# Moving an S5 parameter chain to GpSimd, its output factors to VectorE, and six weight splits into quarters, in a two-layer decoder trunk

## The chip, the cores and the metric

The kernel runs on one core of a Trainium2 chip. The metric is the device time of one launch in microseconds (us), as the median of several runs. The engines of the core are named as in the profile: PE (TensorE, matrix products), PEld (its weight loads), DVE (VectorE), ACT (ScalarE), POOL (GpSimd) and SP (SyncE, which issues the DMAs here). Each engine works through its own queue strictly in order; semaphores hold an instruction until what it reads is there.

## The reference, cut to what matters

The trunk has two residual layers over 1024 positions of width 1024. Layer 0 runs sliding-window attention and an S5 state-space mixer side by side off one input projection; layer 1 is an indexed sparse attention. The change touches the S5 mixer of layer 0 and the preparation of weights.

```python
def s5_mixer(u, log_dt, a_re, a_im, b_re, b_im, c_re, c_im, d_skip, glu_w, glu_b):
    ug = u.reshape(bsz, L, G, W // G)
    dt = jnp.exp(log_dt)[:, None]
    mag = jnp.exp(a_re * dt)
    ang = a_im * dt
    ab_re = mag * jnp.cos(ang)
    ab_im = mag * jnp.sin(ang)
    den = a_re * a_re + a_im * a_im
    n_re = ab_re - 1.0
    n_im = ab_im
    f_re = (n_re * a_re + n_im * a_im) / den
    f_im = (n_im * a_re - n_re * a_im) / den
    bb_re = f_re[..., None] * b_re - f_im[..., None] * b_im
    ...
    bu_re = jnp.einsum('blgh,gph->blgp', ug, bb_re)
    ...
    _, _, x_re, x_im = lax.associative_scan(ssm_combine, (at_re, at_im, bu_re, bu_im), axis=1)
    y = (jnp.einsum('blgp,ghp->blgh', x_re, c_re) - jnp.einsum('blgp,ghp->blgh', x_im, c_im) + d_skip * ug)
    y = jax.nn.gelu(y.reshape(bsz, L, W))
    h = y @ glu_w + glu_b
    return h[..., :W] * jax.nn.sigmoid(h[..., W:])
```

All products with weights are in float32 accuracy: the kernel splits each weight and each activation into a rounded part (hi) and a remainder (lo) and sums three products.

## The kernel before, in words

**Order of the work.** The program is written in one order, and a planner places each engine's instructions by priority (earlier in the program is higher) and by its own estimate of when each is ready; what it fixes is the order in each engine's queue. So an instruction written later can stand earlier in a queue where the planner expects a gap.

**Layer 0, start.** The input comes in eight pieces of 128 rows. For each, ACT rounds it (L336), DVE takes the remainder (L337), ACT squares it (L341), and a running sum of squares is kept (L343, on POOL for pieces 1 and 2, else on DVE). PE meanwhile forms the first chunk of the projection (L357 to L359). Then `mean_square` (L203 to L211) sums over partitions on PE (L208), and takes 1 / rms as a power of -0.5 on POOL (L211); DVE spreads it over a diagonal `dg` (L365), PE multiplies that with ones (L368) and ACT copies the product to `rb` (L369).

**S5's parameters** (L435 to L539) are tiles of 128x16 numbers, all on DVE except the two sines on ACT (L454, L457): `exp_of` (L240 to L253) is an exponential as a polynomial; it gives dt and mag. Angle, its reduction to one turn and the sine and cosine follow, then the input factors `Bb` (L459 to L473, L534 to L539), the powers `pw` of the step (L490 to L500), the table `ue` of powers of the unit rotation, each made by `square` (L493) and straightened by `unit` (L505), and the first 16 steps `T16` of the rotation (L517 to L528).

**Quarters of S5.** `s5_quarter` (L589 to L710) runs four times. Each builds on DVE the input weights `Q` (L613 to L618) and a rotation table `Tb` of 128 steps (L634 to L639), and on POOL the output factors `W` (L620 to L627) by `cmul` (L598 to L610), which four DMAs bring into `Wp` (L632). PE transposes `Q` (L646), multiplies it with the input (L674), DVE rotates the result, runs the scans (L687) and writes the states `X` (L678 to L698). PE then forms the output from `M` and U (L705) and from `Wp` and `X` (L707). `Q`, `W`, `Wp`, `Tb` and `X` have one buffer each. Between and beside the quarters the planner places the other projections of layer 0: keys and values (`proj_rows`, L218 to L220, and `norm_heads`, L383 to L394, whose 1 / rms is on POOL, L199 and L200), the second S5 input chunk, the queries (`q_chunk`, L396) and the gates (`gate_chunk`, L411, `proj_cols`, L232 to L234).

**Weights.** `load_w` (L135) brings each of 39 weight pieces of 128x2048 in; ACT rounds it (L153) and DVE or POOL subtracts (L154). The list `LO_ON_V` says which pieces DVE takes. Pieces of DVE, and of POOL those numbered 21, 31 and 32, are done in steps of 2 of 8 rows (128x512), the others whole (128x2048) where they are flushed at once; from piece 21 on a projection paces the steps itself.

Of the kernel before, what the change touches and what calls it, by code (L numbers as in the profile page):

```python
# [8 lines left out]
F32 = mybir.dt.float32  # L9
# [59 lines left out]
def tile_hybrid_swa_s5_dsa(  # L69
# [56 lines left out]
    LO_ON_V = (0, 1, 2) + tuple(range(13, 21)) + (29, 30) + tuple(range(33, 39))  # L126
# [8 lines left out]
    def load_w(src):  # L135
# [19 lines left out]
        return (hi, lo), [piece, WSTEP if i in LO_ON_V or i in (21, 31, 32) else 8, 0]  # L155
# [39 lines left out]
    last_rstd = [None]  # L195
# [7 lines left out]
    def mean_square(acc, n, r, re):  # L203
# [36 lines left out]
    def exp_of(sp, o, xin, n):  # L240

        a, kf, pl = (sp.tile([128, n], F32, name=f"ex{i}", bufs=2) for i in range(3))
        ki = sp.tile([128, n], I32, name="exi", bufs=2)
        V.tensor_scalar(a, xin, 88.0, -87.0, op0=OP.min, op1=OP.max)
        V.tensor_scalar(kf, a, 1.0 / math.log(2.0), MAGIC, op0=OP.mult, op1=OP.add)
        V.tensor_scalar(kf, kf, MAGIC, None, op0=OP.subtract)
        V.scalar_tensor_tensor(a, kf, -0.693359375, a, op0=OP.mult, op1=OP.add)
        V.scalar_tensor_tensor(a, kf, 0.693359375 - math.log(2.0), a, op0=OP.mult, op1=OP.add)
        V.tensor_scalar(pl, a, 1.0 / 5040.0, None, op0=OP.mult)
        for d_ in (720.0, 120.0, 24.0, 6.0, 2.0, 1.0):  # L250
            V.scalar_tensor_tensor(pl, pl, 1.0 / d_, a, op0=OP.add, op1=OP.mult)
# [183 lines left out]
    with es_sp:  # L435
# [1234 lines left out]
```

## Time and profile before

| | us |
|---|---|
| median of 3 runs | 1075.03 |
| lowest and highest | 1072.58 to 1075.17 |
| the profiled execution, its own time | 1078.34 |
| its span from first to last instruction | 1076.6 |
| PE busy | 1012.1 (94%) |
| DVE busy | 770.3 (72%) |
| ACT busy | 607.1 (56%) |
| POOL busy | 469.0 (44%) |
| mean granted TensorE clock, share of full speed | 0.983 |

Busy shares are means over very different stages, so they don't tell what a change in one stage is worth. For that the table of stages, the waits of PE and the timeline of each engine are read. In a timeline a row is: start, duration (us), engine, line, operation, output <- inputs and shapes, count; in brackets the idle time of the engine just before it and what ended it.

### The profile page before, as it was taken

What the parts mean: (1) busy time and instruction counts of PE and PEld (TensorE: products, weight loads), DVE (VectorE), ACT (ScalarE), POOL (GpSimd) and SP (SyncE); (2) the same over time, 40 slices, a digit from 0 to 9 for tenths busy, and PEclk for the clock granted to TensorE, in tenths of its full rate; (3) what the DMA queues carried; (4) which work ended last, traced back from release to release, by engine and by line L of the source; (5) the groups of instructions that cost most, each with busy time, mean ns of one, the idle gap of its engine ahead of it and who ended that gap; (6) DMA issues with size and microseconds to landing.
All of it is one profiled execution on the core that took longest, in us unless ns stands there. A gap on an engine that the chain in (4) does not pass through costs nothing.

```text
span 1076.6 us, 19055 instructions
## 1 busy us (share of the span) xinstructions
PE 1012.1 (94%) x6536; PEld 888.5 (83%) x6536; DVE 770.3 (72%) x1742; ACT 607.1 (56%) x1609; POOL 469.0 (44%) x647
## 2 busy tenths in 40 slices
PE   6898788999999899999999989999999879999998
PEld 4787788999877478887889989999887659898898
DVE  6999889635677675455469678889877997777742
ACT  6453344324545443444466789879976776565620
POOL 2267677332211212223031577867653947555000
PEclk9999899999999899999999999999999999999999
DMA  7282533594343324652011223022325745665333
GB/s 264 79 265 81 149 103 104 151 269 134 96 140 118 103 103 142 210 196 108 1 40 63 67 74 104 16 80 84 98 89 176 246 130 163 200 190 172 115 104 113
DMA packets 103697, 138.33 MB, mean 128 GB/s; under 512 B 9352, under 2 KB 79880, under 8 KB 98736
## 3 DMA queue, kind: packets, MB, share of 16 engines
q1 hardware_dynamic: 103600, 137.12, 39.9%
q8 instruction: 51, 0.84, 0.3%
q14 instruction: 46, 0.38, 0.1%
HBM read 102.31 MB, written 36.21 MB: 129 GB/s over the span
## 4 chain that ended last, share of the span: by engine, by line
PE 68%; DVE 16%; ACT 5%; DMA 4%; POOL 3%; issue 3%; SPq 1%; ACTq 0%; POOLq 0%; DVEq 0%
PE mm L234 7%; PE mm L232 7%; PE mm L233 7%; PE mm L218 4%; PE mm L219 4%; PE mm L220 4%; PE mm L1546 3%; PE mm L1547 3%; PE mm L1545 3%; PE tr L1396 2%; PE psx L796 2%; DVE tmp L687 1%; PE mm L1411 1%; PE mm L1412 1%; PE pq L1370 1%
## 5 line engine op out<-in xcount | busy, mean ns | idle before, releaser
L154 POOL TENSOR_TENSOR wlo<-wraw,whi 128x512 fp32r<-128x512 f32 (+1 forms) x50 | 101.1, 2047 | 111.6 <-ACT whi L153 106.1
L153 ACT CAST whi<-wraw 128x512 fp32r<-128x512 f32 (+2 forms) x122 | 84.3, 748 | 70.6 <-DMA wraw<-in_wo_dram 28.0
L219 PE MATMUL mm<-wlo,h1T_hi 128*128 128x256 f32 x384 | 109.5, 286 | 0.0
L1369 POOL TENSOR_TENSOR bt<-bt,mk 128x384 f32<-128x384 f32 (+3 forms) x80 | 83.8, 1066 | 59.0 <-DMA bt<-g_d 41.0
L218 PE MATMUL mm<-whi,h1T_hi 128*128 128x256 f32 x384 | 109.0, 286 | 0.2 <-DVE gst L976 0.2
L220 PE MATMUL mm<-whi,h1T_lo 128*128 128x256 f32 x384 | 108.9, 285 | 0.0
L1216 DVE TENSOR_SCALAR_CACHE_REDUCE vjunk<-sc,vt 128x512 bf16<-128x512 uint16 (+5 forms) x90 | 91.0, 1012 | 2.7
L233 PE MATMUL mm<-hT_lo,whi 128*128 128x256 f32 (+1 forms) x288 | 86.4, 300 | 0.0
L234 PE MATMUL mm<-hT_hi,wlo 128*128 128x256 f32 (+1 forms) x288 | 86.1, 299 | 0.0
L232 PE MATMUL mm<-hT_hi,whi 128*128 128x256 f32 (+1 forms) x288 | 86.0, 299 | 0.0
L1252 ACT ACTIVATE sjunk<-sc,st 128x384 bf16<-128x384 uint16 (+5 forms) x90 | 77.7, 864 | 6.8 <-POOL st L1256 4.7
L1545 PE MATMUL mm<-aT_hi,whi 128*128 128x256 f32 x256 | 73.0, 285 | 1.2 <-ACT aT_hi L1519 1.2
L218 PEld LDWEIGHTS mm<-whi,h1T_hi 128*128 128x128 f32 x384 | 72.3, 189 | 1.0 <-PE psi L1060 0.6
L1546 PE MATMUL mm<-aT_lo,whi 128*128 128x256 f32 x256 | 72.2, 282 | 0.7 <-DVE aT_lo L1520 0.7
L219 PEld LDWEIGHTS mm<-wlo,h1T_hi 128*128 128x128 f32 x384 | 72.4, 188 | 0.4
L220 PEld LDWEIGHTS mm<-whi,h1T_lo 128*128 128x128 f32 x384 | 72.2, 189 | 0.4
L1547 PE MATMUL mm<-aT_hi,wlo 128*128 128x256 f32 x256 | 72.1, 282 | 0.0
L391 ACT ACTIVATE st<-mm,nr 128x64 f32<-128x64 f32 (+1 forms) x160 | 45.5, 357 | 45.0 <-POOL nr L200 44.6
L154 DVE TENSOR_TENSOR wlo<-wraw,whi 128x512 fp32r<-128x512 f32 (+1 forms) x72 | 50.2, 737 | 25.3 <-ACT whi L153 22.7
L1067 DVE SCALAR_TENSOR_TENSOR sc<-relu,wi,sc 128x384 f32<-128x384 f32 (+3 forms) x70 | 49.4, 707 | 20.6 <-ACT relu L1062 16.9
L1380 ACT ACTIVATE s<-s,mn 128x384 f32<-128x384 f32 (+7 forms) x56 | 45.9, 820 | 26.9 <-DVE mn L1374 26.8
L1400 DVE TENSOR_TENSOR pT_lo<-tr,pT_hi 128x512 fp32r<-128x512 f32 x72 | 49.1, 685 | 15.7 <-ACT pT_hi L1399 15.6
(396 smaller groups left out, 3483.3 us busy)
## 6 DMA issues: line engine op xcount, KB each, us to landing
wraw<-in_w_dram SPq DMA_DIRECT2D x20, 1024.0 KB, 5.0
wraw<-in_wo_dram SPq DMA_DIRECT2D x16, 1024.0 KB, 5.3
bt<-g_d SPq DMA_DIRECT2D x24, 256.0 KB, 3.9
g_d<-g1r_d SPq DMA_DIRECT2D x8, 576.0 KB, 10.7
bt<-g_d SPq DMA_DIRECT2D x24, 192.0 KB, 3.3
qT_d<-gst SPq DMA_DIRECT2D x32, 128.0 KB, 2.0
qT<-qT_d SPq DMA_DIRECT2D x32, 128.0 KB, 3.2
xh<-in_xT_dram SPq DMA_DIRECT2D x16, 256.0 KB, 3.8
```

The lines of the kernel that those rows point to most:

```text
L153: S.copy(hi[p_], raw[p_])
L154: eng.tensor_sub(lo[p_], raw[p_], rd(hi[p_]))
L218: T.matmul(ps, a, hi[:, k, c0:c1], start=(k == 0), stop=False)
L219: T.matmul(ps, a, lo[:, k, c0:c1], start=False, stop=False)
L220: T.matmul(ps, b, hi[:, k, c0:c1], start=False, stop=(k == 7))
L232: T.matmul(o, a, hT[0][:, k, ts], start=(k == 0), stop=False)
L233: T.matmul(o, a, hT[1][:, k, ts], start=False, stop=False)
L234: T.matmul(o, b, hT[0][:, k, ts], start=False, stop=(k == 7))
L1216: V.tensor_scalar(junk[:, :128 * (b + 1)], data(b), self.thr(j), None, op0=OP.is_ge, op1=OP.add, accum_out=self.cnt[:, it, j:j + 1])
L1545: T.matmul(ps, a, aT[0][:, k, toks], start=(k == 0), stop=False)
L1546: T.matmul(ps, a, aT[1][:, k, toks], start=False, stop=False)
L1547: T.matmul(ps, b, aT[0][:, k, toks], start=False, stop=(k == 7))
```

## The change

Parts of one diff:

- S5's parameters: `exp_of` takes an engine and a way to do "(a op c) op b"; both exponentials, the angle and its reduction, `pw`, `square` and `unit` go to POOL. POOL does "(a op c) op b" as two instructions through the tile `stt_t`. By count of the code 117 instructions leave DVE and 149 come to POOL.
- Behind 1 / rms: what follows the reduction of the angle in this block is issued behind the power of `mean_square` on POOL, behind `dg` on DVE and behind the last copy to `rb` on ACT (`issue_after` puts an edge on each instruction of the same engine in the block). Of POOL's 149 instructions 34 stand ahead of that point and 115 behind it. `mag` is now computed behind it.
- W: `cmul` for `W` on DVE, in 4 steps of 4 instructions per quarter in place of POOL's 20 per quarter, with the temporary tiles `tmp` that `Q` and `Tb` use.
- Weight pieces 9 to 12 are subtracted by DVE; all remaining pieces of POOL in steps of 128x512.

```diff
-    LO_ON_V = (0, 1, 2) + tuple(range(13, 21)) + (29, 30) + tuple(range(33, 39))
+    LO_ON_V = (0, 1, 2) + tuple(range(9, 21)) + (29, 30) + tuple(range(33, 39))
...
-        return (hi, lo), [piece, WSTEP if i in LO_ON_V or i in (21, 31, 32) else 8, 0]
+        return (hi, lo), [piece, WSTEP, 0]
...
-        G.tensor_tensor(r, r, neghalf[:, :n], op=OP.pow)
+        last_rms[0] = G.tensor_tensor(r, r, neghalf[:, :n], op=OP.pow).ins
...
-    def exp_of(sp, o, xin, n):
+    def exp_of(E, stt, sp, o, xin, n):
...
-        V.tensor_scalar(a, xin, 88.0, -87.0, op0=OP.min, op1=OP.max)
+        E.tensor_scalar(a, xin, 88.0, -87.0, op0=OP.min, op1=OP.max)
...
-        exp_of(sp, dt, ldt, 16)
+        stt_t = q16("stt_t")
+
+        def g_stt(o, a, c, b, op0, op1):
+            G.tensor_scalar(stt_t, a, c, None, op0=op0)
+            G.tensor_tensor(o, stt_t, b, op=op1)
+
+        exp_of(G, g_stt, sp, dt, ldt, 16)
...
-        exp_of(sp, mag, tt, 16)
-        V.tensor_mul(ang, aim, dt)
...
+        G.tensor_mul(ang, aim, dt)
...
+        es_late = ExitStack()
+        for i_ in (last_rms[0], dg_mul.ins, rb_copy.ins):
+            es_late.enter_context(tc.issue_after(i_))
+        r2 = q16("r2")
         S.activation(sn, r, AF.Sin)
...
+        S.activation(cs, r2, AF.Sin)
+        exp_of(G, g_stt, sp, mag, tt, 16)
...
         def square(dst, src):
-            V.tensor_mul(small(0), src[:, 0], src[:, 0])
...
+            G.tensor_mul(sg_[0], src[:, 0], src[:, 0])
+            G.tensor_mul(sg_[1], src[:, 1], src[:, 1])
+            G.tensor_sub(dst[:, 0], sg_[0], sg_[1])
+            g_stt(dst[:, 1], src[:, 0], 2.0, src[:, 1], op0=OP.mult, op1=OP.mult)
...
+            G.tensor_mul(sg_[0], e[:, 0], e[:, 0])
+            G.tensor_mul(sg_[1], e[:, 1], e[:, 1])
+            G.tensor_add(sg_[0], sg_[0], sg_[1])
+            G.tensor_scalar(sg_[0], sg_[0], -0.5, 1.5, op0=OP.mult, op1=OP.add)
+            G.tensor_mul(e, e, bc(sg_[0][:, None, :], [128, 2, 16]))
...
+        es_late.close()
...
-        cmul(G, W[:, :, :, 0, :], CT[:, :, js], pw[:, 0, 0, js, None], pw[:, 0, 1, js, None], 16, neg=True)
+        cmul(V, W[:, :, :, 0, :], CT[:, :, js], pw[:, 0, 0, js, None], pw[:, 0, 1, js, None], 16, neg=True)
         for lv, n in enumerate((1, 2, 4)):
...
+            cmul(V, Wf[:, :, :, 16 * n:32 * n], Wf[:, :, :, 0:16 * n], pw[:, lv, 0, js, None], pw[:, lv, 1, js, None],
+                 16 * n, neg=True)
```

## Rows read from the trace of the kernel before

**Rows 1.** Busy time by stage: stage (us from the span's start), its length, then busy us and count of instructions of PE, PEld, DVE, ACT and POOL, granted clock, DMA share, GB/s. The stages are quarter 0 of S5 from POOL's first long subtraction to its X, the quarters 1, 2 and 3, and the projections and the attention behind them.

```profile
73.00:116.00 43.00, 31.49 (x190) 26.34 (x189) 41.28 (x55) 8.76 (x24) 35.71 (x47) 0.91 0.45 128
116.00:145.00 29.00, 25.84 (x220) 24.41 (x219) 24.99 (x55) 12.90 (x73) 19.22 (x28) 0.95 0.41 123
145.00:181.00 36.00, 32.44 (x265) 31.14 (x266) 31.94 (x57) 19.11 (x98) 28.03 (x36) 0.94 0.44 130
181.00:210.00 29.00, 27.28 (x234) 26.41 (x234) 25.55 (x53) 11.88 (x51) 11.10 (x10) 0.95 0.45 120
210.00:290.00 80.00, 80.00 (x626) 75.50 (x625) 35.53 (x124) 28.55 (x81) 17.86 (x7) 0.98 0.57 174
```

**Rows 2.** First, what PE waited for in the first 250 us: total us, times, longest. Then three PE rows of the timeline with the idle time ahead of them: the first state product of quarter 0, and two of the last blocks of the window attention.

```profile
PE ps L707 <- DVE X L698: 11.7, 3, 7.6
...
PE tr L404 <- ACT st L391: 4.1, 3, 1.8
PE tr L368 <- DVE sq L365: 3.6, 1, 3.6
PE ps L705 <- DMA M<-km: 2.2, 1, 2.2
PE ps L358 <- DVE hT_lo L337: 1.9, 1, 1.9
PE ps L646 <- DVE Q L609: 1.7, 1, 1.7
...
114.36 0.80 PE L707 MATMUL ps<-X,Wp 128*128 128x128 f32 x2 [7.63 <-DVE X L698]
...
359.97 1.03 PE L790 MATMUL tr<-ident,s 128*128 128x128 f32 x4 [1.49 <-DVE s L781]
362.01 1.97 PE L796 MATMUL psx<-pT,vt 128*64 128x512 f32 x2 [1.01 <-DVE pT L793]
```

**Rows 3.** The subtractions of POOL in the whole trace (count: shortest, median and longest ns, first and last start, shapes), one of them in the timeline of POOL, and rows of DVE's timeline that stand beside a long one: in quarter 0, and twice in the window attention.

```profile
L154 POOL TENSOR_TENSOR wlo<-wraw,whi x50: 1281/1300/4968, 73.5 to 916.9; 128x512 fp32r<-128x512 f32 x40, 128x2048 fp32r<-128x2048 f32 x10
...
73.49 4.66 POOL L154 TENSOR_TENSOR wlo<-wraw,whi 128x2048 fp32r<-128x2048 f32 x1
...
73.60 4.70 DVE L610 TENSOR_TENSOR Q<-tmp 128x128 f32<-128x128 f32 x1
...
293.26 5.34 DVE L781 TENSOR_SCALAR s<-s,den 128x256 f32<-128x256 f32 x4
...
353.39 4.48 DVE L771 TENSOR_TENSOR sd<-snk,nm 128x4 f32<-128x4 f32 x1
```

**Rows 4.** The start, in the timeline of DVE (a parameter's product and the remainder of input piece 2), of POOL (the two sums of squares, and the power of 1 / rms) and of ACT (the table of the sine).

```profile
13.86 2.36 DVE L459 TENSOR_TENSOR den<-aa 128x16 f32<-128x16 f32 x1
...
18.82 1.28 DVE L337 SCALAR_TENSOR_TENSOR hT_lo<-xt,gain,hT_hi 128x1024 fp32r<-128x1024 f32 x1
...
13.66 5.01 POOL L343 TENSOR_TENSOR acc<-acc,sq 128x1024 f32<-128x1024 f32 x2 [9.82 <-ACT sq L341]
...
43.53 1.71 POOL L211 TENSOR_TENSOR rr<-rr,neghalf 128x8 f32<-128x8 f32 x1 [24.86 <-DVE rr L210]
...
31.69 1.28 ACT L454 ACT_TABLE_LOAD   x1
```

**Rows 5.** Small instructions on POOL, from its timeline: two that hang on each other and a product behind them, a sum of W, and one beside a busy DVE.

```profile
48.92 0.30 POOL L199 TENSOR_SCALAR nr<-nms,rr 128x2 f32<-128x2 f32 x1
49.31 0.72 POOL L200 TENSOR_TENSOR nr<-nr,neghalf 128x2 f32<-128x2 f32 x1
50.02 0.45 POOL L393 TENSOR_TENSOR st<-st,kg 128x128 f32<-128x128 f32 x1
...
68.70 0.83 POOL L199 TENSOR_SCALAR nr<-nms,rr 128x2 f32<-128x2 f32 x1 [2.79 <-ACT st L388]
...
82.06 0.32 POOL L607 TENSOR_TENSOR W<-tmpg 128x64 f32<-128x64 f32 x1
```

**Rows 6.** The four lines of `cmul` between 66 and 210 us, one row for each of L603, L604, L606 and L607: busy us and count of DVE (first two rows only) and of POOL, granted clock, DMA share, GB/s. POOL's are W.

```profile
66.00:210.00 144.00, 16.18 (x24) 12.57 (x20) 0.94 0.46 135
...
66.00:210.00 144.00, 12.44 (x24) 13.23 (x20) 0.94 0.46 135
...
66.00:210.00 144.00, 10.84 (x20) 0.94 0.46 135
...
66.00:210.00 144.00, 12.31 (x20) 0.94 0.46 135
```

**Rows 7.** DVE's timeline: the first rotation of quarter 0, and `cmul` on DVE for quarter 1 at a time when POOL did nothing.

```profile
93.60 0.69 DVE L678 TENSOR_TENSOR tmp<-ps,Tb 128x512 f32<-128x512 f32 x1
...
118.31 0.68 DVE L604 TENSOR_TENSOR tmp<-Q,pw 128x512 f32<-128x512 f32 x1
118.91 0.28 DVE L603 TENSOR_TENSOR tmp<-Tb,ue 128x128 f32<-128x128 f32 x1
119.11 0.28 DVE L604 TENSOR_TENSOR tmp<-Tb,ue 128x128 f32<-128x128 f32 x1
...
119.65 0.42 DVE L610 TENSOR_TENSOR Q<-tmp 128x256 f32<-128x256 f32 x1
119.98 0.22 DVE L609 TENSOR_TENSOR Tb<-tmp 128x64 f32<-128x64 f32 x1
120.12 0.22 DVE L610 TENSOR_TENSOR Tb<-tmp 128x64 f32<-128x64 f32 x1
```

More of the change, by code (lines that the diff above doesn't have):

```diff
@@ L193, in get @@
             return r if n > 1 else r[0]
[L195 removed]
+    last_rstd, last_rms = [None], [None]
     def rstd_of(pool_, ms, n, name, eps):
@@ L368, in tile_hybrid_swa_s5_dsa @@
             T.matmul(pt, ones, dg[:, 4 * half:4 * half + 4].rearrange("p i t -> p (i t)"), start=True, stop=True)
-            S.copy(rb[:, half * 512:(half + 1) * 512], pt)
+            rb_copy = S.copy(rb[:, half * 512:(half + 1) * 512], pt)
     with tc.tile_pool(name="bias0", bufs=1, reuse_waits="tile") as bp:
@@ L484, in tile_hybrid_swa_s5_dsa, with unit @@
         tm = [sp.tile([128, 256], F32, name=f"tm{i}") for i in range(4)]
-        def small(i):
-            return tm[i][:, :16]
         mg, c_, s_ = P5[:, 0], P5[:, 1], P5[:, 2]
-        V.tensor_mul(pw[:, 0, 0], mg, c_)
-        V.tensor_mul(pw[:, 0, 1], mg, s_)
+        sg_ = [q16(f"sg{i}") for i in range(2)]
+        G.tensor_mul(pw[:, 0, 0], mg, c_)
+        G.tensor_mul(pw[:, 0, 1], mg, s_)
         def square(dst, src):
-            V.tensor_mul(small(0), src[:, 0], src[:, 0])
-            V.tensor_mul(small(1), src[:, 1], src[:, 1])
-            V.tensor_sub(dst[:, 0], small(0), small(1))
-            V.scalar_tensor_tensor(dst[:, 1], src[:, 0], 2.0, src[:, 1], op0=OP.mult, op1=OP.mult)
+            G.tensor_mul(sg_[0], src[:, 0], src[:, 0])
+            G.tensor_mul(sg_[1], src[:, 1], src[:, 1])
+            G.tensor_sub(dst[:, 0], sg_[0], sg_[1])
+            g_stt(dst[:, 1], src[:, 0], 2.0, src[:, 1], op0=OP.mult, op1=OP.mult)
         square(pw[:, 1], pw[:, 0])
         square(pw[:, 2], pw[:, 1])
+        def unit(e):
+            G.tensor_mul(sg_[0], e[:, 0], e[:, 0])
[3 more added lines that the diff above has]
+            G.tensor_mul(e, e, bc(sg_[0][:, None, :], [128, 2, 16]))
         square(ue[:, 0], P5[:, 1:3])
@@ L503, in tile_hybrid_swa_s5_dsa @@
         square(ue[:, 0], ue[:, 1])
-        def unit(e):
-            V.tensor_mul(small(0), e[:, 0], e[:, 0])
-            V.tensor_mul(small(1), e[:, 1], e[:, 1])
-            V.tensor_add(small(0), small(0), small(1))
-            V.tensor_scalar(small(0), small(0), -0.5, 1.5, op0=OP.mult, op1=OP.add)
-            V.tensor_mul(e, e, bc(small(0)[:, None, :], [128, 2, 16]))
         unit(ue[:, 0])
@@ L621, in s5_quarter @@
         Wf = W.rearrange("p t j s h -> p t j (s h)")
-        cmul(G, W[:, :, :, 0, :], CT[:, :, js], pw[:, 0, 0, js, None], pw[:, 0, 1, js, None], 16, neg=True)
+        cmul(V, W[:, :, :, 0, :], CT[:, :, js], pw[:, 0, 0, js, None], pw[:, 0, 1, js, None], 16, neg=True)
         for lv, n in enumerate((1, 2, 4)):
-            for a0 in range(0, n, 2):
-                m = min(2, n)
-                cmul(G, Wf[:, :, :, 16 * (n + a0):16 * (n + a0 + m)], Wf[:, :, :, 16 * a0:16 * (a0 + m)],
-                     pw[:, lv, 0, js, None], pw[:, lv, 1, js, None], 16 * m, neg=True)
+            cmul(V, Wf[:, :, :, 16 * n:32 * n], Wf[:, :, :, 0:16 * n], pw[:, lv, 0, js, None], pw[:, lv, 1, js, None],
+                 16 * n, neg=True)
         Wp = s5q.tile([128, 4, 2, 8, 16], F32, name="Wp")
```

42 lines of the change are left out of this document (20 added, 22 removed).

## The prediction

> **What bounds the kernel now.** I read the stage table first. Behind 210 us PE is busy throughout, with 80.00 of 80.00 us; in the four quarters of S5 it is not: 31.49 of 43, 25.84 of 29, 32.44 of 36 and 27.28 of 29 us [rows 1]. That is 43.00 + 29.00 + 36.00 + 29.00 - 31.49 - 25.84 - 32.44 - 27.28 = 20.0 us of idle PE, and the granted clock is 0.91 to 0.95 there. What PE must do ahead of the window attention is fixed, so idle time taken away here comes off the end nearly in full, as long as projections are left to fill in. The table also says who is busy instead: in quarter 0 DVE for 41.28 of 43 us, and POOL for 35.71.
>
> Then PE's waits: for X 11.7 us in three, 7.63 of them in quarter 0; for the scaled queries 4.1, for the DMA of M 2.2, for Q 1.7; and outside the quarters 3.6 on the diagonal of 1 / rms and 1.9 on the remainder of an input piece [rows 2]. Those in the quarters are 11.7 + 4.1 + 2.2 + 1.7 = 19.7, the 20.0 of the table.
>
> Last, why DVE is late: a sum of 128x128 took 4.70 us on DVE from 73.60, just while POOL subtracted 128x2048 for 4.66 us from 73.49; a sum of 128x4 took 4.48 and four scalings 5.34 us in the window attention [rows 3], where such a 128x128 sum or product takes 0.28 [rows 7]. DVE stands still while POOL runs. It works the other way too: a POOL instruction of 0.30 us took 0.83 beside a busy DVE [rows 5].
>
> **The change, part by part.** The sum is made on the profiled execution, 1078.34 us, span 1076.6.
>
> *Start.* DVE's product for `den` took 2.36 us beside POOL's sums, and the remainder of input piece 2 came only at 18.82 [rows 4]; PE waited 1.9 us for it. Nothing of S5 stands there on DVE now; the remainder can go between POOL's two sums (5.01 us for both, so the first ends near 16.2) and be ready near 17.5. The 1.9 us go. Against it: 34 new POOL instructions up to the angle, each of which may hold DVE for its own length; at 0.3 us [rows 5] that is 10 us at most on an engine that feeds PE. DVE gives up its own early parameter work, so I keep -1.9, with ends -2 and +2.
>
> *1 / rms.* Its power takes POOL 1.71 us [rows 4] as before; PE's 3.6 us there stay: 0, with ends -1 and +0.5. The sine's table load (1.28 us) [rows 4] moves on ACT from an idle stretch to behind `rb`, ahead of the keys' norms: hidden, as the sine has to be there only when POOL is through with mag. If not, 1.3 us.
>
> *POOL's chain and quarter 0.* Behind the power (end 45.24) POOL gets 115 small instructions that mostly hang on each other. A step of two such took 49.31 - 48.92 = 0.39 us; an independent sum of 128x64 takes 0.32 [rows 5]. I take 0.36: 115 x 0.36 = 41 us. The planner puts the keys' norms between them, 8 x (0.30 + 0.72 + 0.45) = 12 us [rows 5], and one weight in quarters, 4 x 1.3 = 5 us [rows 3]: 45 + 58 = 103, and with some 7 us of waiting for DVE about 110. Ends: 0.30 us a step, the bare length, and only the norms between, 92; 0.55, about half way to the contended 0.83, 125. The rotation table of quarter 0 needs the last `ue`, so its first rotation, at 93.60 before [rows 7], comes near 112. From there X took 114.36 - 93.60 = 20.8 us [rows 2, 7], some 8 of it standstills (a long subtraction and W) and projection work that is done earlier now; I take 12.5: X near 125, 10 us later than now. That is not yet 10 us of PE: the planner sees a longer chain too, and sets the queries' projections ahead of L707. What PE waits for is only the lateness that the planner does not foresee, the standstills: about 7 on the chain, 4 from a weight; it was about as much before. So PE's 7.63 stay: 0, with ends -8 and +12.
>
> *W to DVE.* POOL loses 12.57 + 13.23 + 10.84 + 12.31 = 49 us [rows 6]. DVE gains, by starts of consecutive instructions, 2 x (2 x 0.20 + 2 x 0.14) + (2 x 0.34 + 2 x 0.20) + (2 x 0.60 + 2 x 0.34) = 4.3 us per quarter, 17 in all [rows 7]. Against that, DVE gets rid of the standstills behind W's pieces. What they cost is between nothing and 6.4 us a quarter: the stage of quarter 2, with W and a weight on POOL (36 instructions), has 31.94 us of DVE, that of quarter 3, with a weight and no W (10 instructions), 25.55 [rows 1]. I take 4, since quarter 1, with W and no weight, has only 24.99. So the move is about even for DVE's load. And the W of quarters 0 and 1 can go into the time in which DVE waits for POOL's chain, 8.6 us. The queries' 1 / rms no longer stands behind W on POOL: PE's 4.1 on L404 go, and the 2.2 on M, whose DMAs stood in SP's queue behind those of Wp, mostly. New on DVE: the sums of W wait for the last DMAs of `Wp`, and the rotation of the same quarter is queued behind them. Together -3, with ends -8 and +5.
>
> *Quarters.* Ten POOL subtractions of the trace are of 128x2048, pieces 3 to 12; the other 40 are of 128x512 already [rows 3], so quarters are new for pieces 3 to 8 only. Four take 4 x 1.3 = 5.2 us instead of 4.66: DVE stands still as long in total, but has a turn between. 0, ends -3 and +2.
> The Trainium skill (SBUF — State Buffer, "Who interferes with whom") says that the port pair that both engines use is locked for a whole instruction by whichever starts first, and the other blocks fully. The trace agrees with 4.70 beside 4.66 us. By that rule alone, cutting an instruction in four changes only how long one wait is.
>
> *Pieces 9 to 12 to DVE.* In the window attention's end the 4.48 us standstill sits right ahead of PE's waits of 1.49 and 1.01 [rows 2, 3]. In its place come four subtractions of the size of 0.6 us by start (a 128x512 row) [rows 7], 2.4 us, spread. The four scalings of 5.34 us lose 4 too. PE has other work in most of that: -2, with ends -4 and +1.
>
> Sum: -1.9 + 0 + 0 - 3 + 0 - 2 = -6.9, so 1071.4 for the profiled execution. The median of the runs stands at 1075.03 / 1078.34 = 0.997 of it: 1068.
>
> **The rivals.**
>
> *GpSimd's chain becomes the bound (slower).* The 115 steps take 0.55 us rather than 0.36, because DVE's own Q, W and Bb run beside them: 63 + 17 + 45 = 125. Quarter 0's X then comes near 140. The planner's order is kept in the queues, so PE waits at L674 or L707 for what it did not foresee: 125 - 110 = 15 us more, less what it gains elsewhere (7). 1078.34 - 7 + 15 = 1086, median 1083. For it: 0.83 where 0.30 would do [rows 5]. Against: DVE has little to do between 50 and 70 us once its parameters are gone. It decides from a last `ue` at about 117 us: up to there the gain elsewhere covers it.
> The Trainium skill (GPSIMD Engine Reference, "Engine selection") says elementwise work belongs on VectorE, as GpSimd takes about twice the time for two inputs. The rows agree (1.3 us for a 128x512 difference, 0.68 for a product of that size on DVE) [rows 3, 7]. It speaks against the first part of this change, and this rival is what it would do here.
>
> *Relief in full (faster).* The waits of the quarters mostly go: of 19.7 us, 5 stay. -14.7 - 1.9 - 2 = -18.6: 1059.7, median 1057. For it: POOL's 49 us of W and their standstills are what DVE loses most in quarter 0. Against: the chain is new.
>
> *Nothing comes of it (same).* The planner's new order puts the same amount of waits elsewhere: gains at the start and in the attention are real, 4 us, and the quarters give them back. 1075 +- 3. The quarters of S5 are filled with projections; if X comes later than they last, PE waits there.
>
> *It doesn't do what it says:* where the planner puts the parameters late on POOL behind norms, they are not ahead of need. That is within the first rival.
>
> **How the numbers follow.** A measurement of this kernel tells 0.3%, 3.2 us, from no change. Chances: the forecast (1063 to 1073, nearly all faster) 0.40; relief in full 0.13; same 0.22; GpSimd's chain 0.25, of which 0.03 end within 0.3%. Faster: 0.36 + 0.13 = 0.49; same 0.04 + 0.17 + 0.03 = 0.24; slower 0.05 + 0.22 = 0.27. The likeliest one's own range is 1063 to 1073. The range for 8 in 10 reaches from near the full relief to the chain's price: 1058 to 1083.
>
> **What would show it.** Right: no idle PE near 20 us; the last `ue` on POOL between 100 and 117 us; L707 of quarter 0 with 5 to 10 us of idle ahead; no more L404 waits behind POOL; no DVE row over 2 us in the quarters; no sum of 4 us near 353. Wrong: an idle PE of over 12 us in quarter 0 (GpSimd's chain), or under 8 us in all four quarters (relief in full). A DVE that waits for the DMA of Wp over 2 us would be a cost that I set at nothing.

## The result, and the profile after

| | before | after |
|---|---|---|
| median of 7 runs each, on one chip | 1075.89 us | 1067.98 us |
| lowest to highest | 1072.58 to 1078.13 | 1061.44 to 1069.93 |
| ratio after / before, 95% interval | | 0.9918 (0.9896 to 0.994) |
| the profiled execution, its span | 1078.34, 1076.6 | 1064.1, 1062.4 |
| PE busy, idle in the span | 1012.1, 64.5 | 1008.0, 54.4 |
| granted clock of that execution | 0.983 | 0.992 |

The kernel is 0.8% faster; 1068 was predicted. The profiled execution of after is one of its shortest: its seven runs lie between 1061.44 us at a clock of 0.994 and 1069.93 at 0.984. So of the 14.2 us between the two profiled executions, 10.1 are idle PE (64.5 - 54.4) and 4.1 are PE's busy time (1012.1 - 1008.0), at a higher granted clock (0.992 against 0.983). Idle PE is what I compare below, and medians where a time is meant.

The stages of [rows 1] in the kernel after (stage, length, busy us of PE, PEld, DVE, ACT, POOL, clock, DMA share, GB/s):

```profile
73.00:116.00 43.00, 40.84 (x291) 36.45 (x290) 33.76 (x90) 17.35 (x87) 30.17 (x81) 0.96 0.43 125
116.00:145.00 29.00, 27.23 (x224) 26.50 (x223) 28.20 (x68) 17.76 (x88) 16.63 (x17) 1.00 0.53 149
145.00:181.00 36.00, 34.84 (x319) 33.61 (x317) 32.11 (x76) 15.78 (x71) 12.73 (x14) 1.00 0.52 146
181.00:210.00 29.00, 26.81 (x211) 25.87 (x210) 28.54 (x61) 6.80 (x12) 6.41 (x4) 0.94 0.32 102
210.00:290.00 80.00, 76.87 (x621) 75.37 (x621) 47.83 (x140) 25.18 (x72) 12.76 (x8) 0.96 0.61 166
```

From 73 to 210 us PE is idle for 7.3 us, where it was 20.0. Behind 210, where it was busy throughout, 3.1 us have appeared. PE's waits of the first 250 us, answering to [rows 2]:

```profile
PE ps L651 <- DVE Q L616: 4.8, 3, 2.2
PE tr L369 <- DVE sq L365: 2.3, 1, 2.3
...
PE ps L712 <- DVE X L703: 2.1, 3, 1.3
PE ps L358 <- DVE hT_lo L337: 0.9, 1, 0.9
```

X fell from 11.7 us to 2.1, the queries' transposes and M are gone from the list, and Q grew from 1.7 to 4.8. Yet X does not come earlier. DVE's timeline of after: the remainders at the start; the first product of `Bb` (L543); the last projection product of `uT` ahead of quarter 0 (L566); the first step of Q (L622); the first rotation (L683); and X (L703):

```profile
13.84 7.77 DVE L337 SCALAR_TENSOR_TENSOR hT_lo<-xt,gain,hT_hi 128x1024 fp32r<-128x1024 f32 x3 [0.71 <-ACT hT_hi L336]
...
85.42 0.45 DVE L543 TENSOR_TENSOR tm<-Bt,P 128x256 f32<-128x256 f32 x1
...
89.53 1.19 DVE L566 TENSOR_TENSOR uT<-mm,rb 128x512 f32<-128x512 f32 x1 [1.90 <-PE mm L234]
90.64 1.71 DVE L622 COPY Q<-Bb 128x128 f32<-128x128 f32 x1
...
113.31 0.69 DVE L683 TENSOR_TENSOR tmp<-ps,Tb 128x512 f32<-128x512 f32 x1
...
124.90 3.45 DVE L703 TENSOR_TENSOR X<-tmp 64x512 f32<-64x512 f32 x2
```

X of quarter 0 ends at 128.35 us, 13.2 later than at 113.48 + 1.69 = 115.17 before, and PE waits 0.3 us for it and not 7.63: its queue holds projections ahead of L712. POOL's timeline has the power of 1 / rms 4 us earlier than in [rows 4], and the last `ue` at 90 us; its steps start 0.3 us apart:

```profile
39.48 2.22 POOL L211 TENSOR_TENSOR rr<-rr,neghalf 128x8 f32<-128x8 f32 x1
...
89.21 0.22 POOL L515 TENSOR_TENSOR sg<-sg,sg 128x16 f32<-128x16 f32 x1
89.52 0.20 POOL L516 TENSOR_SCALAR sg<-sg 128x16 f32<-128x16 f32 x1
89.81 0.25 POOL L517 TENSOR_TENSOR ue<-ue,sg 128x32 f32<-128x32 f32 x1
```

All of POOL's subtractions are now short (compare [rows 3]; count, then shortest, median and longest ns):

```profile
L154 POOL TENSOR_TENSOR wlo<-wraw,whi x64: 1270/1300/2279, 67.6 to 901.8; 128x512 fp32r<-128x512 f32 x64
```

### The profile page after: what moved, and what is told of

The parts are those of the page before. It is cut to its first block, busy times and chain, and to the rows that moved or that the text cites. A ratio compares the mean times of both kernels' runs of the same rounds, so it can differ in the third digit from the quotient of the medians.

```text
span 1062.4 us, 19148 instructions
## 1 busy us (share of the span) xinstructions
PE 1008.0 (95%) x6536; PEld 885.1 (83%) x6536; DVE 749.0 (71%) x1705; ACT 609.5 (57%) x1639; POOL 451.0 (42%) x730
## 4 chain that ended last, share of the span: by engine, by line
PE 62%; DVE 14%; ACT 7%; DMA 6%; POOL 5%; issue 4%; SPq 1%; ACTq 0%; DVEq 0%; POOLq 0%
PE mm L234 8%; PE mm L232 7%; PE mm L233 7%; PE mm L218 4%; PE mm L219 4%; PE mm L220 4%; PE mm L1551 2%; PE mm L1552 2%; PE mm L1550 2%; PE psx L801 2%; PE tr L1401 2%; PE mm L1416 1%; DMA wraw<-in_wo_dram 1%; DVE s L1379 1%; PE tr L795 1%
## 5 line engine op out<-in xcount | busy, mean ns | idle before, releaser
L153 ACT CAST whi<-wraw 128x512 fp32r<-128x512 f32 (+1 forms) x152 | 87.1, 640 | 73.1 <-PE mm L233 37.6
L154 POOL TENSOR_TENSOR wlo<-wraw,whi 128x512 fp32r<-128x512 f32 x64 | 87.4, 1394 | 94.2 <-ACT whi L153 88.7
L232 PE MATMUL mm<-hT_hi,whi 128*128 128x256 f32 (+1 forms) x288 | 86.3, 300 | 0.0
L154 DVE TENSOR_TENSOR wlo<-wraw,whi 128x512 fp32r<-128x512 f32 (+1 forms) x88 | 60.9, 736 | 14.5 <-ACT whi L153 11.9
L919 POOL TENSOR_TENSOR acc<-acc,sq 128x512 f32<-128x512 f32 x12 | 18.0, 1502 | 101.8 <-DVE wlo L154 60.4
## 6 DMA issues: line engine op xcount, KB each, us to landing
g_d<-g1r_d SPq DMA_DIRECT2D x8, 576.0 KB, 10.5
```

The costliest lines, as they stand in the source:

```text
L153: S.copy(hi[p_], raw[p_])
L154: eng.tensor_sub(lo[p_], raw[p_], rd(hi[p_]))
L232: T.matmul(o, a, hT[0][:, k, ts], start=(k == 0), stop=False)
```

## The experiments

The theory at this point: what PE gained in the quarters comes from DVE and POOL no longer standing in each other's way (W, long subtractions), not from the parameters and not from an earlier S5. Rivals: it is the start (1 / rms earlier), it is one of the three parts alone, or it is when the parameters run rather than where. The first question was what each part does by itself and in company, so all eight combinations of the three parts stand here, then the variants. "Params" is the first two points of the change together.

| kernel | ratio to before, 95% | idle PE 0 to 73 | 73 to 210 | 210 to 400 | 400 to end |
|---|---|---|---|---|---|
| before | 1 | 13.6 | 20.0 | 5.6 | 25.4 |
| e1 params | 1.002 (1.0003 to 1.0038) | 13.6 | 19.2 | 6.9 | 26.3 |
| e2 W | 0.9965 (0.9947 to 0.9983) | 13.0 | 9.5 | 12.8 | 26.0 |
| e3 weights | 0.9976 (0.9956 to 0.9996) | 13.8 | 13.2 | 5.1 | 26.2 |
| e6 params + W | 0.9939 (0.992 to 0.9958) | 12.6 | 8.9 | 13.4 | 24.8 |
| e9 params + weights | 0.9913 (0.989 to 0.9936) | 13.2 | 13.4 | 3.5 | 23.3 |
| e5 W + weights | 0.991 (0.988 to 0.9939) | 13.7 | 6.9 | 8.4 | 25.1 |
| after, all three | 0.9918 (0.9896 to 0.994) | 11.9 | 7.3 | 8.8 | 26.5 |
| e4 after, not held | 1.0013 (0.9993 to 1.0033) | 20.5 | 5.5 | 7.6 | 24.0 |
| e7 params held, on DVE | 0.9915 (0.9885 to 0.9945) | 12.4 | 8.2 | 6.3 | 27.1 |
| e10 W + pieces 9 to 12 | 0.9882 (0.986 to 0.9904) | 13.0 | 7.2 | 8.8 | 24.6 |
| e11 W + quarters | 0.9907 (0.9884 to 0.993) | 13.4 | 8.0 | 8.0 | 24.8 |
| e8 after, Bb first | 0.9889 (0.986 to 0.9918) | 13.5 | 7.0 | 6.4 | 24.5 |
| e12 e8, sums on DVE | 0.9869 (0.984 to 0.9897) | 12.8 | 6.5 | 8.0 | 25.6 |

Idle PE is the length of a stage less PE's busy time in the stage view of that kernel's one profiled execution, as in the rows quoted below. The last stage moves between 23.3 and 27.1 us with no visible relation to the edits, so a single difference of some 3 us is not read by itself. PE's busy time differs too, from 1007.9 us (e10) to 1018.3 (e7, whose profiled execution was its longest, 1074.0), so idle PE and time don't move one for one. Each edit also makes the planner lay out every queue anew: e5, e7, e8 and after, which differ in the parameters and Bb alone, lie between 0.9889 and 0.9918 at intervals that overlap. So a difference of 0.3% or less may come from the order alone.

**e1, the parameters alone.** The kernel after with W and the weights of before:

```diff
-            cmul(V, Wf[:, :, :, 16 * n:32 * n], Wf[:, :, :, 0:16 * n], ...
+                cmul(G, Wf[:, :, :, 16 * (n + a0):16 * (n + a0 + m)], ...
...
-    LO_ON_V = (0, 1, 2) + tuple(range(9, 21)) + (29, 30) + tuple(range(33, 39))
+    LO_ON_V = (0, 1, 2) + tuple(range(13, 21)) + (29, 30) + tuple(range(33, 39))
...
-        return (hi, lo), [piece, WSTEP, 0]
+        return (hi, lo), [piece, WSTEP if i in LO_ON_V or i in (21, 31, 32) else 8, 0]
```

> Kernel before with the first part alone: the parameters on GpSimd, held behind 1 / rms. W stays on GpSimd and the weights stay whole. The sum of the prediction gives this part -1.9 at the start and 0 in quarter 0: 1074, ratio 0.998. If the whole gain is that the start's engines are free of parameters (1 / rms comes 4 us earlier in the trace of after), it is here alone: 1067, ratio 0.992. If GpSimd's queue is what decides, W of quarter 0 now stands behind the 115 steps on GpSimd, whose last table step then comes after 95 us and whose W after 105: idle PE in quarter 0 over 12 us, 1080 or more, ratio over 1.004.

1078.52 us: slower by 0.2%, between the first and the third case, and small enough for a new order alone to make it. 1 / rms came as early as in after (its power at 39.95), so an earlier 1 / rms is not the gain. What it cost is seen in quarter 1, in POOL's and PE's timelines:

```profile
135.28 4.59 POOL L154 TENSOR_TENSOR wlo<-wraw,whi 128x2048 fp32r<-128x2048 f32 x1
...
145.58 0.58 POOL L616 TENSOR_TENSOR W<-tmpg 128x64 f32<-128x64 f32 x1 [5.44 <-DMA Wp<-W]
...
146.90 1.10 POOL L200 TENSOR_TENSOR nr<-nr,neghalf 128x4 f32<-128x4 f32 x1
```

```profile
148.61 0.88 PE L405 MATMUL tr<-ident,st 128*128 128x128 f32 x2 [9.50 <-ACT st L392]
```

The queries' 1 / rms (L200) is queued behind a long subtraction, and behind a sum of W that waits 5.44 us for a DMA to free its target; PE stands 9.50 us at the end of that line (and 5.3 us once for an X). W and the norms share POOL's queue in the kernel before too; as I read it, the parameters pushed W back until it met them. Below, e9, with W on POOL, keeps such waits, and e6, with W on DVE, has none.

**e2, W alone.** The kernel before with

```diff
-                cmul(G, Wf[:, :, :, 16 * (n + a0):16 * (n + a0 + m)], ...
+            cmul(V, Wf[:, :, :, 16 * n:32 * n], Wf[:, :, :, 0:16 * n], ...
```

> Kernel before with W on VectorE alone. The sum of the prediction gives it -3: 1073, ratio 0.997, with the waits for the scaled queries (4.1 us) and for M (2.2 us) gone and the wait of 7.6 us for X of quarter 0 still there. If the gain is the start's, nothing: 1076, ratio 1.000. If W's share of GpSimd is what holds VectorE in the quarters, most of the gain is here: 1068, ratio 0.993. If VectorE is the bound of the quarters (41.28 of 43 us busy in quarter 0), its 4.3 us a quarter more are seen: over 1078, ratio over 1.002.

1072.82 us, a third of a per cent, as predicted in size (-3, or 0.997). The place was not as predicted. The stages 73 to 210 and 210 to 400 us, of before, then of e2:

```profile
73.00:210.00 137.00, 117.05 (x904) 108.30 (x903) 123.75 (x217) 52.64 (x243) 94.06 (x118) 0.94 0.44 126
210.00:400.00 190.00, 184.44 (x1176) 150.59 (x1176) 115.17 (x313) 82.73 (x213) 41.51 (x15) 0.97 0.45 141
```

```profile
73.00:210.00 137.00, 127.53 (x1022) 118.97 (x1021) 127.33 (x286) 56.54 (x249) 47.77 (x42) 0.99 0.49 140
210.00:400.00 190.00, 177.17 (x1104) 144.49 (x1103) 124.03 (x318) 83.99 (x212) 43.22 (x15) 0.97 0.44 136
```

In the quarters PE gets 10.5 us more work done (117.05 to 127.53); behind 210 us 7.3 are given back (184.44 to 177.17). 5.94 of these are one wait, in the attention: POOL's scaling of `s` (L773 here, L778 before) comes late. It is queued behind a long subtraction, and the sum `den` that it needs stands 4.41 us on DVE beside that subtraction. POOL's rows of e2, DVE's, then PE's:

```profile
341.51 6.43 POOL L154 TENSOR_TENSOR wlo<-wraw,whi 128x2048 fp32r<-128x2048 f32 x1 [22.05 <-ACT whi L153]
348.54 1.92 POOL L773 TENSOR_TENSOR s<-s,den 128x1024 f32<-128x1024 f32 x1 [0.59 <-DVE nm L765]
```

```profile
343.55 4.41 DVE L770 TENSOR_TENSOR den<-den,sd 128x4 f32<-128x4 f32 x1
```

```profile
350.51 1.76 PE L785 MATMUL tr<-ident,s 128*128 128x128 f32 x7 [5.94 <-POOL s L773]
```

Such a subtraction stood in the attention before, too, beside DVE's 4.48 us of [rows 3]; PE's waits right behind it were 1.49 and 1.01 [rows 2]. Its row in POOL's timeline of before:

```profile
352.88 4.97 POOL L154 TENSOR_TENSOR wlo<-wraw,whi 128x2048 fp32r<-128x2048 f32 x1 [6.33 <-ACT whi L153]
```

As I read it, what had covered it are projections, and these are done earlier now. One of the three product lines of the gates and of `uT` (L232) in three stages, PE's busy us and count, before, in e2 and in after:

```profile
0.00:210.00 210.00, 20.21 (x58) 10.92 (x58) 0.94 0.48 149
...
290.00:400.00 110.00, 18.48 (x63) 11.90 (x63) 0.97 0.36 118
```

```profile
0.00:210.00 210.00, 30.67 (x96) 18.11 (x96) 0.97 0.51 155
...
290.00:400.00 110.00, 14.48 (x48) 9.05 (x48) 0.97 0.33 111
```

```profile
0.00:210.00 210.00, 37.08 (x118) 22.27 (x119) 0.98 0.51 158
...
290.00:400.00 110.00, 5.65 (x18) 3.21 (x17) 1.00 0.35 104
```

With the other two lines, after has some 3 x 12.8 = 38 us less of projections between 290 and 400 us than before, so what is slow there is seen. In e2's wait list the queries' L404 is gone, M fell from 2.2 to 1.0, and X from 11.7 to 7.9, its longest from 7.6 to 3.6; I had expected that one to stay.

**e3, the weights alone.** The kernel before with

```diff
-    LO_ON_V = (0, 1, 2) + tuple(range(13, 21)) + (29, 30) + tuple(range(33, 39))
+    LO_ON_V = (0, 1, 2) + tuple(range(9, 21)) + (29, 30) + tuple(range(33, 39))
...
-        return (hi, lo), [piece, WSTEP if i in LO_ON_V or i in (21, 31, 32) else 8, 0]
+        return (hi, lo), [piece, WSTEP, 0]
```

> Kernel before with the weight subtractions alone: pieces 9 to 12 on VectorE, the others of GpSimd in quarters. The sum of the prediction gives it 0 in the quarters and -2 in the attention: 1074, ratio 0.998. If a long hold of the port costs more than its length (the subtraction of 4.66 us stands on quarter 0's chain, and PE waited 7.6 us right behind), quartering alone brings 4 us or more: 1071, ratio 0.995, with no row of over 3 us on VectorE in quarter 0. If not, 1076, ratio 1.000.

1073.11 us, 0.24%: the time is the first case's. The trace is nearer to the second: PE's wait for X falls from 11.7 us in three to 2.3, and the idle time of the quarters by 6.8 us, where the sum had 0 (the waits for M and Q grow, from 2.2 to 4.0 and from 1.7 to 3.2). This kernel's DVE queue around X of quarter 0 has the same order as before, so the two can be laid side by side. DVE before, with POOL's row beside it:

```profile
108.87 4.58 DVE L603 TENSOR_TENSOR tmp<-Q,pw 128x128 f32<-128x128 f32 x1
113.48 1.69 DVE L698 TENSOR_TENSOR X<-tmp 64x512 f32<-64x512 f32 x2
```

```profile
108.36 4.94 POOL L154 TENSOR_TENSOR wlo<-wraw,whi 128x2048 fp32r<-128x2048 f32 x1
```

and e3, DVE, then POOL, then PE:

```profile
107.66 0.69 DVE L603 TENSOR_TENSOR tmp<-Q,pw 128x128 f32<-128x128 f32 x1
108.39 3.33 DVE L698 TENSOR_TENSOR X<-tmp 64x512 f32<-64x512 f32 x2
```

```profile
108.17 3.00 POOL L154 TENSOR_TENSOR wlo<-wraw,whi 128x512 fp32r<-128x512 f32 x2
```

```profile
110.10 0.49 PE L707 MATMUL ps<-X,Wp 128*128 128x128 f32 x2 [0.17 <-DVE X L698]
```

Before, the product of 0.28 us ahead of X stood 4.3 us longer behind one hold of 4.94; now the two X rows lose 1.6 us, and half of X is out in time for PE. The total of POOL's holds hasn't shrunk. DVE takes its turn between them, and the rows on the chain lose 1.6 us in place of 4.3. The Trainium skill (SBUF — State Buffer, "Who interferes with whom") states the hold for a whole instruction; these rows agree (4.58 beside 4.94). This is a kernel with W on POOL; e10 below shows that with W and pieces 9 to 12 on DVE the cut of pieces 3 to 8 brought nothing more.

The time fell less (2.6 us) than the idle PE (6.3 over the span). It is so in the two profiled executions as well: the span fell by 2.2 us, and PE's busy time rose from 1012.1 to 1016.2 at the same mean clock, 0.983. Why it rose stays open.

**e5, e6, e9, the pairs.** Each is after with one part undone: in e5 the parameters as in before, in e6 the weights, in e9 W, by the diffs above.

> Kernel before with W on VectorE and the weights as in after; the parameters stay on VectorE, not held. The two parts alone gave 0.9965 and 0.9976. If the parts add, this gives 0.994 (1069.5), and the parameters, which alone cost 0.2%, bring the remaining 0.2% of after only in W's absence from GpSimd. If the parameters on GpSimd are what makes after fast once W is gone from there, this stays near W alone, 0.9965 (1072). If the parameters are a loss in any company, this is faster than after, under 0.991 (1066).

> Kernel after with the weights as before (pieces 9 to 12 on GpSimd, whole subtractions). Parts that add: 1.002 x 0.9965 = 0.9985 (1074). If W had only been in the way of the parameters' chain on GpSimd (waits of 9.5 us for the queries and of 5.3 us for X where it stays there), the two together bring nearly all of after: 0.993 to 0.994 (1069). A long subtraction of over 4 us beside quarter 0 would then still be seen as a standstill of VectorE.

> Kernel after with W back on GpSimd (its 20 instructions a quarter and its own scratch): parameters on GpSimd and held, weights as in after. With the parameters and W both on GpSimd and whole weights the run was at 1.002; W, its port and the norms of the queries share one queue. If W in GpSimd's queue is what holds the queries and X, this stays at 1.000 (1075 to 1077), with a wait of several us of PE for the scaled queries. If the 9.5 us there came mostly from the long subtraction of 4.59 us ahead of the norms, quarters shorten it: 0.996 (1071).

e5 1067.03, e6 1069.77 and e9 1067.07 us. The parts don't add: e9 would be 1.002 x 0.9976 = 0.9996 and is 0.9913; e6 would be 0.9985 and is 0.9939, as its second case had it. For e5 it isn't shown: it would be 0.994 and is 0.991, and the intervals of the three runs leave room for both. Either pair with the weights brings what all three bring; e6, without them, has 0.9939, and its interval overlaps after's. Beside a relieved POOL the parameters cost nothing there, and bring nothing either: e5, without them, is level with after. In e9 PE still waits 10.2 us for the queries behind W, in four waits where e1 had one of 9.50:

```profile
PE tr L405 <- ACT st L392: 10.2, 4, 4.0
```

Both cases expected there were wrong all the same: the time is after's. Idle PE from 210 to 400 us is only 3.5 in this kernel, for time lost in the quarters leaves projections over for the attention (56 of L232's from 290 to 400 us, where after has 18): the mirror image of e2.

Summed from 73 to 400 us the pattern is plainer. Idle PE is 25.5 before and 26.1, 22.3 and 18.3 with params, W and weights alone; 22.3, 16.9 and 15.3 in e6, e9 and e5; 16.1 in after. Weights take off 6.2 to 9.2 us in any company, W 0.8 to 3.8, the parameters between 1.3 and -0.8. Only the weights' share is clear of the 3 us that I don't read singly; W's shows in e2's time.

**e10, e11, the two halves of the weights, each on top of e2.** e10:

```diff
-    LO_ON_V = (0, 1, 2) + tuple(range(13, 21)) + (29, 30) + tuple(range(33, 39))
+    LO_ON_V = (0, 1, 2) + tuple(range(9, 21)) + (29, 30) + tuple(range(33, 39))
```

and e11:

```diff
-        return (hi, lo), [piece, WSTEP if i in LO_ON_V or i in (21, 31, 32) else 8, 0]
+        return (hi, lo), [piece, WSTEP, 0]
```

> Kernel before with W on VectorE (0.9965 by itself) and pieces 9 to 12 on VectorE; GpSimd's pieces 3 to 8 stay whole. W with both weight edits gave 0.991. The prediction has the gain of the weights in these four pieces, at the attention's end: 0.992 (1067), with no wait of 5.9 us for s there. If it is in the quarters: 0.996 (1072).

> Kernel before with W on VectorE and GpSimd's subtractions, pieces 3 to 12, in quarters; no piece changes its engine. The prediction gives quarters 0: 0.9965 (1072). If a standstill of VectorE costs by its length and not by the sum of them, this one has most of the 0.991: 0.992 (1067), with the idle PE of the S5 quarters near 7 us as against 9.5 us with W alone.

1063.8 and 1066.49 us: each half by itself brings what both do. From e2's 12.8 us between 210 and 400, 8.8 and 8.0 are left, and from 9.5 in the quarters 7.2 and 8.0. The quarters' part isn't read: the pieces that e10 moves come only behind 280 us, and its quarters changed by 2.3 us all the same. The 5.94 us on `s` are gone in both; in e10 DVE has that piece, in e11 it is cut. As the two remove the same wait, their gains don't add.

e10 also corrects e3. Its four subtractions in the quarters are whole, and DVE stands still beside them as before, yet no kernel with these pieces cut is faster beyond the noise. POOL's row, DVE's beside it, and PE's wait for that X:

```profile
136.95 4.66 POOL L154 TENSOR_TENSOR wlo<-wraw,whi 128x2048 fp32r<-128x2048 f32 x1 [2.84 <-ACT whi L153]
```

```profile
137.21 4.95 DVE L689 TENSOR_TENSOR tmp<-tmp,Tb 128x512 f32<-128x512 f32 x1
```

```profile
144.07 0.79 PE L702 MATMUL ps<-X,Wp 128*128 128x128 f32 x2 [2.94 <-DVE X L693]
```

Only one more wait for X of that size is in e10's list, 3.6 us in quarter 3. With W off POOL a long hold costs PE some 3 us where it falls on X, and the kernel is no slower for it; in the kernel before, with W on POOL, the wait was 7.63. e5 is e10 with pieces 3 to 8 cut in quarters: 0.991 against 0.9882, at intervals that overlap. So the cut of these six pieces is worth nothing that shows once W is on DVE and pieces 9 to 12 too.

**e4, not held.** The kernel after without the three edges:

```diff
-        for i_ in (last_rms[0], dg_mul.ins, rb_copy.ins):
-            es_late.enter_context(tc.issue_after(i_))
```

> Kernel after without the three edges that hold the parameters behind 1 / rms; who does what is as in after. If the order behind 1 / rms is what brings 1 / rms forward and with it the gain, this one loses it: the power of 1 / rms on GpSimd comes at 43 us or later, 1072 to 1078, ratio to before 0.996 to 1.002. If it is the freed VectorE that counts and not the order, it is within 0.3% of after: 1065 to 1071; the table of rotations is then ready earlier than at 90 us, and if quarter 0's chain mattered it would be under 1065.

1076.74 us: the first case. POOL's and PE's rows, then stages of e4:

```profile
54.51 1.67 POOL L211 TENSOR_TENSOR rr<-rr,neghalf 128x8 f32<-128x8 f32 x1
```

```profile
57.50 2.93 PE L369 MATMUL tr<-sq,ones 128*128 128x512 f32 x3 [8.34 <-DVE sq L365]
```

```profile
42.00:44.00 2.00, 0.73 (x4) 0.76 (x4) 1.39 (x3) 0.21 (x1) 1.74 (x4) 0.77 0.01 4
44.00:46.00 2.00, 2.00 (x11) 2.00 (x11) 0.00 (x0) 0.00 (x0) 1.49 (x7) 0.50 0.00 0
46.00:57.00 11.00, 3.16 (x12) 2.67 (x12) 4.68 (x20) 2.96 (x10) 10.16 (x34) 0.50 0.00 0
...
60.00:64.00 4.00, 4.00 (x18) 3.21 (x17) 3.05 (x9) 2.94 (x16) 3.83 (x16) 0.55 0.53 221
64.00:68.00 4.00, 4.00 (x36) 4.00 (x35) 3.75 (x14) 3.63 (x29) 3.51 (x17) 1.00 0.53 146
```

The power stands 15 us later behind the chain in POOL's queue, and PE waits 8.34 us. Its clock had fallen to 1.2 GHz, the lower of its two levels (0.50), by 44 us, ahead of that wait and behind two of 0.67 and 2.16 us; it stays there through the wait and near it until about 64 us, while PE is busy again. So the edges are what makes a chain of 149 instructions on POOL bearable: without them the ratio is 1.0013 in place of 0.9918, 1% more.

**e7, when without who.** After with every line of the chain back on DVE, under the same edges:

```diff
-        G.tensor_mul(tt, are, dt)
-        G.tensor_mul(ang, aim, dt)
...
+        V.tensor_mul(tt, are, dt)
+        V.tensor_mul(ang, aim, dt)
...
-            g_stt(dst[:, 1], src[:, 0], 2.0, src[:, 1], op0=OP.mult, op1=OP.mult)
+            V.scalar_tensor_tensor(dst[:, 1], src[:, 0], 2.0, src[:, 1], op0=OP.mult, op1=OP.mult)
```

> Kernel after with the parameter chain on VectorE, but held behind 1 / rms by the same three edges: when without who. If what counts is that nothing of S5 stands ahead of 1 / rms, this keeps after's gain: 1 / rms comes by 41 us and the time is 1065 to 1071. If it is VectorE's load that counts, the chain's 117 instructions of about 0.2 us (23 us) now stand ahead of the keys' and of uT's work on VectorE from 42 us on: PE waits at the first transposes of the keys or at Q, 1074 or more.

1066.79 us, as after, though 1 / rms did not come by 41: its power starts at 43.09, and in e5 at 42.81, about where it stood before (43.53). So the earlier 1 / rms of after isn't needed for its time. With W and the weights changed, the chain may stand on DVE early (e5), on DVE late (e7) or on POOL late (after). Only on POOL and not held does it cost.

**e8, Bb first.** After with L541 to L548 moved ahead of the chain:

```diff
         tm = [sp.tile([128, 256], F32, name=f"tm{i}") for i in range(4)]
...
+        tmv = [t.rearrange("p (j h) -> p j h", h=16) for t in tm]
+        V.tensor_mul(tmv[0], Bre, fr)
...
+        V.tensor_add(Bb[:, 1], tmv[2], tmv[3])
```

> Kernel after with one block moved: the input factors Bb are written ahead of the chain of ue and T16 and not behind, so that they take the four shared scratch tiles first; nothing else changes. In the trace of after Bb waits until 85.4 us for these tiles although its inputs are there at 56.7, and Q and W of quarter 0 start at 90.6, while VectorE is busy for 9.09 of 28 us. With Bb near 57 to 60, Q and W of quarter 0 (16 us) go into that gap. If quarter 0's X then comes 5 to 13 us earlier and this matters to PE: 1060 to 1065, ratio 0.986 to 0.991. If PE's queue is filled with projections in any case, so that an earlier X moves nothing: 1066 to 1070, as after.

1064.67 us, within the first case's range, but the reason given was wrong. In DVE's timeline of e8 `Bb` is done at 59 us, and Q starts where it did:

```profile
58.73 0.41 DVE L505 TENSOR_TENSOR Bb<-tm,tm 128x256 f32<-128x256 f32 x1
...
89.98 1.20 DVE L567 TENSOR_TENSOR uT<-mm,rb 128x512 f32<-128x512 f32 x1 [4.03 <-PE mm L234]
91.08 1.67 DVE L623 COPY Q<-Bb 128x128 f32<-128x128 f32 x1
```

Q is queued behind the last `uT`, which waits for PE. The scratch tiles were not what held it, and X of quarter 0 is no earlier (its last two rows start at 125.33, in after at 124.90). That e8 is faster than after isn't shown: the intervals overlap.

**e12, e8 with the first sums of squares on DVE:**

```diff
-                    (G if k < SQ_G else V).tensor_add(acc, acc, sq)
+                    V.tensor_add(acc, acc, sq)
```

> The kernel with Bb ahead of T16, and in addition the sums of squares of input pieces 1 and 2 on VectorE (1.2 us each) in place of GpSimd (2.4 and 3.4 us, beside which three remainders of VectorE took 7.74 us). If these two standstills still cost PE something at the start, 1 to 2 us off: 1063, and 1 / rms a little earlier. If VectorE's sums only take the place of its standstills, as the Bb kernel alone: 1064 to 1067. Slower than 1068 if the sums now hold back the remainders that PE needs.

1063.65 us, ratio 0.9869 (0.984 to 0.9897). 1 / rms comes at 38.02 in place of 40.27. The 1.0 us against e8 can't be told from nothing. It has the lowest ratio of all, and e10 (0.9882), which leaves the parameters where they were, is the simplest of the fast ones; both beat before clearly, and after by 0.4 to 0.5% at intervals that touch or overlap.

## Why the prediction was right, and where only its sum was

1068 was predicted and 1067.98 measured. That the two are so close is luck: several terms were wrong, and their errors cancelled.

*Start, -1.9.* Idle PE up to 73 us fell from 13.6 to 11.9 in after, and the wait for the remainder from 1.9 to 0.9. POOL's steps did cost there what was feared (some took 1.1 us, and three remainders 7.77), within the bounds. But as a part of the whole the move is worth nothing that shows: without it (e5) the time is the same, 0.991 against 0.9918. Mis-sized: about 0, not -1.9.

*1 / rms, 0.* PE's wait there fell from 3.6 to 2.3 us, a little past the end of -1; the power comes 4 us earlier.

*POOL's chain, 0.* The outcome was right (no loss, in company), the steps were wrong against each other. The last `ue` was put at 110 and came at 90: the chain starts 3.5 us earlier, the steps start 0.3 us apart and not 0.36, and there was almost no waiting for DVE, which was busy for 9.09 of 28 us from 45 to 73. That gain was lost again: "the W of quarters 0 and 1 can go into the time in which DVE waits for POOL's chain" failed, since Q and W stand behind `uT` in DVE's queue. So the first rotation came at 113.31 (112 was predicted) and PE's first product with that X at 127.03 (125). X was later and the wait for it shorter, as PE's queue had been filled with projections: that part of the argument held, and more strongly than I counted on, for the 7.63 us did not stay.

*W to DVE, -3.* Measured by itself -0.35%, 3.8 us, inside the bounds. Idle PE makes it up differently: 10.5 us gained in the quarters and 7.3 lost behind them. What failed is the condition on which idle time taken away "comes off the end nearly in full, as long as projections are left to fill in". Fewer were left (48 products of L232 in place of 63 from 290 to 400 us), and in the attention PE stood for 5.94 us in one wait. The DVE wait for the DMA of `Wp` that was set at nothing did not appear: no such wait is in DVE's list of after.

*Quarters, 0.* As a term of this sum the 0 stands: with W on DVE and pieces 9 to 12 there, cutting pieces 3 to 8 brings nothing that shows (e10 to e5, 0.9882 to 0.991). The reason given for it failed: PE doesn't pay for DVE's standstill by its total length. With the weights alone, idle PE in the quarters fell by 6.8 us, and the rows at 108 us show how. On top of W, cutting all ten pieces is worth 6 us of time (e2 to e11, 1072.82 to 1066.49), by the attention more than by S5.

*Pieces 9 to 12, -2.* The place was right, the size was not. On top of W they are worth 9 us of time (1072.82 to 1063.8), 4 of them idle PE between 210 and 400 us, where the long hold stood without cover; once it is cut in quarters anyway, they add nothing (e11 against e5). In after the two waits that I named are smaller (1.2 and 0.3 us) and others are new (a DMA of `qT`, 3.1 us, and `sg` of L881, 2.3).

So the total was right because terms set too low (the weights, 0 and -2) made up for one that brought nothing (the start). The sum also took the parts as independent, and they are not: by the measured ratios e2 and e3 alone account for 0.6%, any pair with the weights for 0.9%, and all three for 0.8%. Of the signs named ahead, two for the forecast failed: the last `ue` came before 100 us, and L707's wait in quarter 0 was 0.3 us, not 5 to 10. Of the rivals, *GpSimd's chain becomes the bound* was right that the chain can cost, 0.2% in e1 and all of the gain in e4, but by another way than slow steps and a late last `ue`: by what else stands in POOL's queue, W and the norms in e1, 1 / rms in e4. The Trainium skill (GPSIMD Engine Reference, "Engine selection") advises against elementwise work on GpSimd; here no run shows a gain from moving the parameters there; e1 shows a loss of 0.2%, and e4 is 1% slower than after. *Relief in full* was to be seen by under 8 us of idle PE in all four quarters; it was 7.3. By that sign this rival had the quarters right and the forecast had not, and yet the time fell by 8 us, not by 18. In the two profiled executions idle PE fell by 12.7 us in the quarters and by 1.8 at the start, but grew by 3.2 from 210 to 400 us, where the rival had -2, and by 1.1 behind.

## What to carry to other kernels

- Idle PE that is filled with later work is a loan: before counting it in full, look at what that work was going to cover, above all single long holds of a shared port: one in the attention cost PE 2.5 us before and 5.9 in e2, where fewer projections were left to cover it.
- Price the parts of a change in company. Edits that remove the same waits don't add (in e10 and e11 each half of the weights brought all of it), and an edit that costs a little alone (a chain put ahead of W and norms in one queue) may be free once the others are made.
- When a moved chain shares a queue with one urgent instruction, hold the chain behind it: here that edge was worth 1%.

## What the runs showed of the hardware that was not expected

- POOL's small instructions depend on who else works: dependent steps of 128x16 took 0.20 to 0.25 us at the end of the chain of after, at 89 us, and at its start, while DVE subtracted and summed tiles of 128x1024, seven of them between 16 and 33 us took 1.10 to 1.14 us.
- A wait of PE can cost more than its length. In e4 the granted clock was at 0.50 through the wait of 8.34 us, and behind it at 0.50 from 57 to 60 us and 0.55 from 60 to 64 while PE worked for 2.50 and 4.00 us: by an estimate from these rows some 3 us of work at full clock lost. The clock had fallen before that wait, and it fell in after at the same point (0.50 from 44 to 46 us); there PE waited for 2.3 us only, and it was back at 0.99 from 46 to 50.
